# Where the hidden layer's combinations are made: behind the pair, or within the next pair's products

## The chip, the core and the metric

The kernel runs on one core of a Trainium2 chip. A core has a matrix engine (TensorE, PE in the profile, with its weight loads as PEld), a vector engine (VectorE, DVE), an activation engine (ScalarE, ACT), a general engine (GpSimd, POOL) and a queue engine (SyncE, SP), which here issues the DMAs. Each engine runs its own instructions in order, and they wait for one another by semaphores. The metric is the device time of one execution, in microseconds.

## The reference

One layer of an encoder is applied to two groups of tokens, a sample (512 tokens) and a prompt (1024 tokens), each with 16 meta tokens in front:

```python
def encoder_layer(x, w_in, ..., g_mlp, w_up, w_down):
    h = rmsnorm(x, g_mix)
    z = h @ w_in
    ...
    x = x + mixed @ w_out
    a = jax.nn.relu(rmsnorm(x, g_mlp) @ w_up)
    return x + (a * a) @ w_down
```

The change concerns `a` and `a * a` for the prompt: 1024 tokens of 1024 channels, times W_up (1024 by 4096), then relu and square.

## The kernel before

**Arithmetic.** Matrices are in 32-bit floats. Each operand is split into a rounded part (hi) and a rest (lo), and a product is the sum of three matmuls, hi·hi, hi·lo and lo·hi (`mm3`). For the prompt, both multiplications of the MLP are made by blocks of two by two with seven block products instead of eight (the scheme of Strassen and Winograd). The blocks' sums and differences have to be made: those of the normalised input and of the weights before the products, and those of the products after them.

**The class `Halves`** does this for the prompt. The tokens are two halves of 512 (TH), the channels two halves of 512. `up` (L1370) goes over 16 pairs of blocks of W_up (g), 256 hidden channels each. A pair has seven products of 12 matmuls with 512 columns, in this order: b11 (bank ps_mm), s2·t2 (ps_s), s3·t3 (ps_o), s1·t1 (ps_t), b21 (into ps_mm again), s4·b22 (added into the bank of s1, ps_t) and a22·t4 (added into the bank of s3, ps_o). Below they are called b11, s2, s3, s1, b21, s4 and the last.

**Behind the products** the outputs of a pair are put together in two tiles of 128x1024, r and r_ (in the profile r_hi and r_lo, two buffers each):
- L1391, ACT: b11's bank is copied into r.
- L1394, DVE, three times: the sums with the banks of s2, s3 and s1, each written into r_. The third reads ps_t, into which s4 is then accumulated.
- L1398, ACT: relu of ps_mm after b21.
- L1401, DVE: the sum with ps_t after s4; L1404, DVE: the sum with ps_o after the last product.
- L1407 and L1408, ACT: relu of r's right half and of r_.
- L1411, DVE: the squares of r and of r_, in place; L1412, SP: each is stored to DRAM.
- L1417, DVE: four combinations (h) of the quarters of r and r_, 128x512 each, which are operands of the block products of W_down; L1419, SP: two DMAs that store them. The two tiles of h have one buffer each.

**The weights of the next pair** are made beside the products. `prepare` (L1338) is a generator whose steps `up` takes between the products. Each step issues casts on ACT (`high`, L1286) and subtractions on POOL (`low` and `combine`, all of them L1283), and the last one the fetch of the pair after (L1280, SP). Per pair POOL has ten instructions: one of 128x1024 and nine of 128x512.

**Order.** A scheduler orders the instructions of each engine by the order of the program and by what is ready. `layer.pinned()` puts the instructions within it behind the last one traced so far on their own engine. The steps of `prepare` are pinned. The combinations are not: one of them (r's left less its right half) runs ahead of L1404 in the profile, the other three behind the square of r_.

After the loop `start_down` and `down` take over: W_down reads squares and combinations back from DRAM.

## Time and profile before

| what | us |
|---|---|
| median of three runs | 2049.44 |
| lowest and highest | 2048.82, 2049.87 |
| the profiled execution | 2049.82 |
| its span, first to last instruction | 2047.7 |
| matmuls (PE) busy in it | 1960.9 |
| DVE busy | 1131.1 |
| POOL busy | 987.6 |
| ACT busy | 756.1 |
| four combinations, first to last start | 1440.7 to 1736.9 |

The profile is of one execution. Its page gives the busy time of the engines, the span in 40 slices and the chain of work that ended last. Further views list instructions in order of time ("timeline"), who waited for whom ("waits"), and stretches of the span side by side. A row of a timeline has the start and the duration in us, the engine, the line in the kernel, the operation, what it writes and reads, shapes and count, and in brackets the idle time before it with what ended that. Tile names are the program's; since buffers are taken in turns, a weight may stand under names such as x, y or gain.

The stage with the edit takes some 310 us of the span, from 1421 to 1732 us for PE.

### The profile page before, as it was taken

The page shows a single profiled execution, that of the slowest core. Times are in us where ns is not written, and L with a number is a line of the kernel's source. Part 1 is how long each engine was busy: PE and PEld are TensorE (multiplying, and loading weights), DVE is VectorE, ACT ScalarE, POOL GpSimd, SP SyncE. Part 2 cuts the span into 40 slices and gives each one's busy share as a digit, 9 for nine tenths or more (in the row PEclk, how much of TensorE's full clock was granted, in tenths as well). Part 3 has the DMA queues.
Part 4 walks back from the last instruction along what each step waited for, and adds up shares of the span by engine and source line. Part 5 has one row for each costly group of instructions (what it writes and reads, how often), then busy time and mean ns, then how long its engine had stood idle before and what let it go on. Part 6 is the DMA issues. An engine that isn't in the chain of part 4 may idle for free.

```text
span 2047.7 us, 26413 instructions
## 1 busy us (share of the span) xinstructions
PE 1960.9 (96%) x9611; PEld 1629.3 (80%) x9611; DVE 1131.1 (55%) x1899; ACT 756.1 (37%) x1322; POOL 987.6 (48%) x758
## 2 busy tenths in 40 slices
PE   6789998999999999999999999999999999999997
PEld 4677876888888878888888888787788788888886
DVE  6573445666665543556664134657777677442246
ACT  3464323333333221555562213114333333433342
POOL 3343535367667751333334225203787885544442
PEclk9889999999999999999999999999999999999999
DMA  6554783245543444545555544312445444976663
GB/s 207 159 138 161 210 244 100 96 133 168 179 147 124 158 166 169 162 116 131 148 178 167 132 111 149 114 62 83 161 148 195 148 171 165 315 236 203 195 192 123
DMA packets 275363, 325.97 MB, mean 159 GB/s; under 512 B 42840, under 2 KB 197208, under 8 KB 274680
## 3 DMA queue, kind: packets, MB, share of 16 engines
q1 hardware_dynamic: 261504, 303.40, 46.5%
q0 software_dynamic: 13728, 20.88, 4.3%
q8 instruction: 76, 1.25, 0.3%
q14 instruction: 55, 0.45, 0.1%
HBM read 235.41 MB, written 91.37 MB: 160 GB/s over the span
## 4 chain that ended last, share of the span: by engine, by line
PE 82%; DVE 7%; DMA 3%; issue 3%; POOL 2%; ACT 2%; SPq 1%; DVEq 0%; ACTq 0%; POOLq 0%
PE ps_mm L128 22%; PE ps_o L128 20%; PE ps_s L128 18%; PE ps_t L128 7%; PE ps_mm L487 3%; PE ps_mm L488 3%; PE ps_mm L489 3%; PE ps_o L617 2%; PE ps_t L600 1%; DVE hn L863 1%; DVE gate L868 1%; POOL w_lo L152 1%; DMA w_raw<-in_w_out 1%; PE ps_t L193 1%; PE ps_s L587 1%
## 5 line engine op out<-in xcount | busy, mean ns | idle before, releaser
L152 POOL TENSOR_TENSOR w_lo<-w_raw,w_hi 128x1024 fp32r<-128x1024 f32 x99 | 248.0, 2511 | 291.3 <-ACT w_hi L151 258.0
L151 ACT CAST w_hi<-w_raw 128x1024 fp32r<-128x1024 f32 x100 | 104.7, 1048 | 170.8 <-PE ps_s L128 48.1
L1046 DVE TENSOR_TENSOR relu<-relu 128x512 f32<-128x512 f32 (+1 forms) x34 | 67.1, 1974 | 108.3 <-ACT relu L1045 108.2
L487 PE MATMUL ps_mm<-hT,w_hi 128*128 128x512 f32 (+3 forms) x312 | 122.7, 393 | 0.0
L489 PE MATMUL ps_mm<-hT,w_lo 128*128 128x512 f32 (+3 forms) x312 | 113.2, 363 | 0.0
L488 PE MATMUL ps_mm<-hT,w_hi 128*128 128x512 f32 (+3 forms) x312 | 113.2, 363 | 0.0
L1283 POOL TENSOR_TENSOR x<-w_hi,x 128x512 fp32r<-128x512 f32 (+1 forms) x42 | 78.5, 1870 | 22.8 <-ACT x L1286 22.8
L594 ACT ACTIVATE sc<-sc,ast 128x288 f32<-128x288 f32 (+4 forms) x96 | 53.8, 561 | 79.5 <-DVE ast L592 79.2
L152 POOL TENSOR_TENSOR w_lo<-r,w_hi 128x1024 fp32r<-128x1024 f32 x15 | 36.0, 2400 | 95.1 <-ACT w_hi L151 95.1
L617 PEld LDWEIGHTS ps_o<-pt,vb 104*64 104x64 f32 (+6 forms) x576 | 64.4, 169 | 12.0 <-ACT pt L132 3.8
L617 PE MATMUL ps_o<-pt,vb 104*64 104x128 f32 (+6 forms) x576 | 66.8, 252 | 5.7 <-ACT pt L132 2.9
L557 POOL TENSOR_TENSOR vb<-vr,vb 96x384 fp32r<-96x384 f32 (+4 forms) x48 | 47.9, 1012 | 49.7 <-ACT vb L556 49.5
L152 POOL TENSOR_TENSOR w_lo<-w_hi 128x1024 fp32r<-128x1024 f32 x18 | 46.5, 2581 | 49.8 <-ACT w_hi L151 45.8
L128 PE MATMUL ps_t<-gate,x 128*128 128x512 f32 x264 | 65.4, 397 | 2.7 <-DVE r_lo L1394 2.6
L152 POOL TENSOR_TENSOR w_lo<-w_lo,w_hi 128x1024 fp32r<-128x1024 f32 x18 | 45.9, 2550 | 45.5 <-ACT w_hi L151 45.5
L600 PE MATMUL ps_t<-ident,sc 128*104 128x128 f32 (+3 forms) x288 | 49.9, 284 | 18.7 <-DVE pt L133 14.1
L489 PEld LDWEIGHTS ps_mm<-hT,w_lo 128*128 128x128 f32 x312 | 60.1, 193 | 8.3
L592 DVE CUSTOM_DVE_ANT_0 sc<-ps_s,bm 128x288 f32<-128x288 f32 (+4 forms) x96 | 46.3, 483 | 36.5 <-PE ps_s L588 15.7
L128 PE MATMUL ps_mm<-gate,x 128*128 128x512 f32 x256 | 64.2, 395 | 0.0
L701 POOL MEMSET bm<- 64x96 f32 (+2 forms) x64 | 12.4, 194 | 105.9 <-DVE ast L592 79.9
L487 PEld LDWEIGHTS ps_mm<-hT,w_hi 128*128 128x128 f32 x312 | 60.6, 194 | 2.2
L488 PEld LDWEIGHTS ps_mm<-hT,w_hi 128*128 128x128 f32 x312 | 60.6, 194 | 2.2
(670 smaller groups left out, 5880.4 us busy)
## 6 DMA issues: line engine op xcount, KB each, us to landing
w_raw<-in_w_in SPq DMA_DIRECT2D x56, 512.0 KB
w_raw<-in_w_up SPq DMA_DIRECT2D x34, 512.0 KB
wt<-hn SPq DMA_DIRECT2D x32, 512.0 KB
hidden_prompt<-h SPq DMA_DIRECT2D x32, 512.0 KB
w_hi<-hidden_prompt SPq DMA_DIRECT2D x20, 512.0 KB
w_raw<-hidden_prompt SPq DMA_DIRECT2D x18, 512.0 KB
w_lo<-hidden_prompt SPq DMA_DIRECT2D x18, 512.0 KB
w_raw<-in_w_out SPq DMA_DIRECT2D x16, 512.0 KB
```

What stands on the lines that cost most here:

```text
L128: self.nc.tensor.matmul(out, a, b, start=(i == 0 and not more), stop=(i == len(terms) - 1), skip_group_check=more)
L151: nc.scalar.copy(out=hi, in_=raw)
L152: (lo_engine or nc.gpsimd).tensor_tensor(out=lo, in0=raw, in1=hi.bitcast(F32), op=ALU.subtract)
L487: nc.tensor.matmul(ps, a[0], b[0], start=(kt == 0), stop=False)
L488: nc.tensor.matmul(ps, a[0], b[1], start=False, stop=False)
L489: nc.tensor.matmul(ps, a[1], b[0], start=False, stop=(kt == 7))
L557: nc.gpsimd.tensor_tensor(out=lo, in0=vs, in1=hi.bitcast(F32), op=ALU.subtract)
L594: nc.scalar.activation(out=sc[:, :W], in_=sc[:, :W], func=AF.Exp, bias=st[:, 0:1], scale=-1.0, accum_out=st[:, 1:2])
L600: nc.tensor.transpose(tp[:ck, c * 128:(c + 1) * 128], sc[:, c * ck:(c + 1) * ck], self.ident)
L617: nc.tensor.matmul(po[:m, j * 128:(j + 1) * 128], v, x, start=(i == 0), stop=(i == len(ops) - 1))
L1046: nc.vector.tensor_tensor(out=r, in0=r, in1=r, op=ALU.mult)
L1283: self.nc.gpsimd.tensor_tensor(out=to, in0=x, in1=y, op=op)
```

## The change

The four combinations and their two stores move from the end of a pair's turn into a function of their own, `combine_hidden`. A pair puts its r, r_ and DRAM place on a list. In the next pair's turn, the first pass of the loop over s2, s3 and s1 calls the function right behind the first L1394 sum (that of s2). The call takes the entry off the list, so the two other passes do nothing. The sixteenth pair's combinations are made behind the loop. Within the function everything is pinned: the combinations come behind the last DVE instruction traced, which is that first sum, and the stores behind the last one on SP. No instruction, shape or buffer changes.

```diff
     def up(self, mp):
         layer, nc, TH = self.layer, self.nc, self.TH
+        late = []
         for g in range(self.NF // 2):
...
                 bank[k] = layer.psum(tag)
                 self.product(bank[k], s[k], 0, q)
                 nc.vector.tensor_tensor(out=to, in0=acc, in1=bank[k], op=ALU.add)
+                for _ in late[:1]:
+                    self.combine_hidden(*late.pop())
                 step()
...
             for i, x in enumerate((r, r_)):
                 nc.vector.tensor_tensor(out=x, in0=x, in1=x, op=ALU.mult)
                 nc.sync.dma_start(to[:, i * 2 * TH:(i + 1) * 2 * TH], x)
+            late.append((r, r_, to))
+        self.combine_hidden(*late.pop())
+
+    def combine_hidden(self, r, r_, to):
+
+        nc, TH = self.nc, self.TH
+        left, right = slice(0, TH), slice(TH, 2 * TH)
+        with self.layer.pinned():
             h = [self.tile(f"h{i}") for i in range(2)]
             s1, s2, s3, s4 = (x[:, y] for x in h for y in (left, right))
             for k, x, y, op in ((s1, r[:, right], r_[:, right], ALU.add), (s2, s1, r[:, left], ALU.subtract),
                                 (s3, r[:, left], r[:, right], ALU.subtract), (s4, r_[:, left], s2, ALU.subtract)):
                 nc.vector.tensor_tensor(out=k, in0=x, in1=y, op=op)
             for i, x in enumerate(h, 2):
                 nc.sync.dma_start(to[:, i * 2 * TH:(i + 1) * 2 * TH], x)
```

## The prediction, made before the change was run

> **What bounds the kernel now.** I read the page first: its line of engines and its chain.

> ```profile
> PE 1960.9 (96%) x9611; PEld 1629.3 (80%) x9611; DVE 1131.1 (55%) x1899; ACT 756.1 (37%) x1322; POOL 987.6 (48%) x758
> PE 82%; DVE 7%; DMA 3%; issue 3%; POOL 2%; ACT 2%; SPq 1%; DVEq 0%; ACTq 0%; POOLq 0%
> ```

> TensorE (PE) is busy 96% of the span and is 82% of the chain, so a change on VectorE (DVE) counts only where PE waits for DVE. The edited stage, W_up of the prompt, has the combinations (L1417) from 1440.7 to 1737.6 us. Next come two stretches of it (columns: us, then busy us and count of PE, weight loads, DVE, ACT, POOL, then granted clock, DMA share, GB/s) and, for 1425 to 1745 us, all waits of PE and of its weight loads, as total, times, longest.

> ```profile
> 1440.00:1460.00 20.00, 17.36 (x75) 13.73 (x74) 15.28 (x14) 6.62 (x10) 15.97 (x10) 1.00 0.43 154
> 1480.00:1500.00 20.00, 20.00 (x88) 16.08 (x87) 14.23 (x11) 6.82 (x11) 16.01 (x10) 1.00 0.45 159
> ...
> PE ps_t L128 <- DVE r_lo L1394: 2.6, 1, 2.6
> PEld ps_t L128 <- DVE r_lo L1394: 4.7, 8, 3.1
> ```

> PE is full except in the stage's second pair (1440 to 1460), where it waits once, 2.6 us, for a sum of L1394; seven more weight loads share the other 1.6 us (4.7 - 3.1). So this edit can win about 3 us at most, and can lose wherever it makes the third L1394 sum later: PE's sixth product of a pair accumulates into the bank which that sum reads (ps_t). The timelines of one undisturbed pair give the clockwork; PE first, then DVE:

> ```profile
> 1496.42 2.96 PE L128 MATMUL ps_mm<-gate,x 128*128 128x512 f32 x12
> ...
> 1507.62 2.96 PE L128 MATMUL ps_mm<-gate,x 128*128 128x512 f32 x12
> 1510.42 2.95 PE L128 MATMUL ps_t<-gate,y 128*128 128x512 f32 x12
> ...
> 1495.24 1.99 DVE L1411 TENSOR_TENSOR r_hi<-r_hi 128x1024 f32<-128x1024 f32 x1 [0.70 <-ACT r_hi L1407]
> 1497.26 1.66 DVE L1417 TENSOR_TENSOR h<-r_hi 128x512 f32<-128x512 f32 x1
> 1498.84 0.68 DVE L1404 TENSOR_TENSOR r_lo<-r_lo,ps_o 128x512 f32<-128x512 f32 x1
> 1500.64 1.23 DVE L1411 TENSOR_TENSOR r_lo<-r_lo 128x1024 f32<-128x1024 f32 x1 [1.13 <-ACT r_lo L1408]
> 1501.90 2.77 DVE L1417 TENSOR_TENSOR h<-r_hi,r_lo 128x512 f32<-128x512 f32 x1
> 1504.70 1.67 DVE L1417 TENSOR_TENSOR h<-h,r_hi 128x512 f32<-128x512 f32 x1
> 1506.40 1.67 DVE L1417 TENSOR_TENSOR h<-r_lo,h 128x512 f32<-128x512 f32 x1
> 1507.99 0.67 DVE L1394 TENSOR_TENSOR r_lo<-r_hi,ps_s 128x512 f32<-128x512 f32 x1
> 1508.77 0.69 DVE L1394 TENSOR_TENSOR r_lo<-r_lo,ps_o 128x512 f32<-128x512 f32 x1
> 1509.56 0.69 DVE L1394 TENSOR_TENSOR r_lo<-r_lo,ps_t 128x512 f32<-128x512 f32 x1
> ```

> Products start every 2.80 us (1510.42 - 1507.62): b11 1496.42, then s2 1499.22, s3 1502.02, s1 1504.82, b21 1507.62, s4 1510.42, the last 1513.21, the next pair at 1516.00. DVE does the previous pair's combinations first and reaches the three sums late, the third ending at 1510.25, 0.17 us before s4 starts. Since s4's weight load is among those that waited, while the product itself is on its 2.80, this is just in time: **slack zero**.

> Why do combinations take 1.67 us? In the sixteenth pair, without POOL beside them, they take 0.69 (last row). GpSimd (POOL) now, the same pair as above:

> ```profile
> 1494.83 1.31 POOL L1283 TENSOR_TENSOR gain<-w_lo,gain 128x512 fp32r<-128x512 f32 x1
> ...
> 1501.62 2.49 POOL L1283 TENSOR_TENSOR y<-w_hi,x 128x1024 fp32r<-128x1024 f32 x1 [3.26 <-ACT x L1286]
> 1504.19 1.62 POOL L1283 TENSOR_TENSOR w_hi<-w_hi,w_lo 128x512 f32<-128x512 f32 x1
> 1505.89 1.62 POOL L1283 TENSOR_TENSOR w_lo<-w_lo 128x512 f32<-128x512 f32 x1
> 1507.48 1.74 POOL L1283 TENSOR_TENSOR x<-w_hi,x 128x512 fp32r<-128x512 f32 x1
> ...
> 1514.43 1.29 POOL L1283 TENSOR_TENSOR x<-w_lo,x 128x512 fp32r<-128x512 f32 x1
> 1515.67 2.27 POOL L1283 TENSOR_TENSOR x<-w_hi,x 128x512 fp32r<-128x512 f32 x1
> ...
> 1720.02 0.69 DVE L1417 TENSOR_TENSOR h<-r_lo,h 128x512 f32<-128x512 f32 x1
> ```

> POOL's instructions end at 1504.11, 1505.81 and 1507.51, the combinations at 1504.67, 1506.37 and 1508.07, always 0.56 later, and each POOL instruction then ends 1.14 after the combination. The two alternate, one combination per POOL instruction, every 1.70 us. The sums of L1394 and L1404, which read PSUM, keep 0.67 to 0.69 beside a busy POOL.

> **The change part by part.** Nothing is added or removed: 4 DVE instructions and 2 DMAs for each of 16 pairs. Fifteen times they move behind the next pair's first L1394 sum; the sixteenth stays behind the loop, where PE already runs W_down, and I cost it at nothing.

> *The tail gets longer.* Ahead of the third sum stood, behind the first blocked combination (ends 1504.67), two combinations and three sums. Now it is three combinations and two sums: the combination that ran early, at 1497.26, joins the row (+1.70) and the first sum leaves it (-0.78, from 1507.99 to 1508.77). Net **+0.92 us**.

> *The row starts earlier.* With that combination gone from between L1411 and L1404, L1404 starts earlier, and behind it ACT's relu and cast and POOL's first instruction, the 128x1024 one, which ended 5.27 us after L1404 began (1504.11 - 1498.84). How much earlier is set by what L1411 waits for. Its input comes 0.20 + 0.69 + 0.70 us after the sixth product's end; POOL's last instruction then holds it off. That one hangs on ACT:

> ```profile
> 1510.62 0.60 ACT L1398 ACTIVATE r_hi<-ps_mm 128x512 f32<-128x512 f32 x1 [3.62 <-PE ps_mm L128]
> 1511.11 0.61 ACT L1286 CAST x<-w_hi 128x512 fp32r<-128x512 f32 x1
> 1513.41 0.69 DVE L1401 TENSOR_TENSOR r_hi<-r_lo,ps_t 128x512 f32<-128x512 f32 x1 [3.16 <-PE ps_t L128]
> ```

> L1398 waits for b21's end, and the cast behind it ends at 1511.72. So POOL, which will be ahead of where it is now, stops there, starts its last three at 1511.80, 1513.05 and 1514.30 (a pitch of 1.25) and ends at 1515.60. L1411 is ready at 1514.8, waits for that, and ends 1.09 later (now 1497.23, against 1496.14 of POOL's first row), at 1516.69. L1404 starts 0.08 before this, 0.61 after the next pair's b11, where it is 2.42 now (1498.84 - 1496.42). If this pair itself stalled by x at its sixth product, the next b11 moves by x and POOL's gate does not: 0.61 - x, but not under 0.20, when L1404's own bank is finished (as L1398 starts 0.20 after s4's start).

> POOL's 128x1024 then ends at 0.61 - x + 5.27 = 5.88 - x after b11. The first sum runs from 1502.22 to 1502.89, 6.47 after b11, so the first combination misses that gap: it meets POOL's *second* instruction (0.08 + 1.29 us more), which ends at 7.25 - x. Today it waits until 7.69 (1504.11). Gain 0.44 + x, at most 0.85.

> *Per pair.* Stall = 0.92 - 0.44 - x = 0.48 - x, not under 0.07, with x the stall of the pair before: alternately 0.07 and 0.41, **mean 0.24 us**. Over 13 pairs (third to fifteenth) +3.1. In the sixteenth, combinations take 0.69 (no POOL work left), three of them fit, and nothing is lost.

> *The second pair* has its own wait now:

> ```profile
> 1440.74 0.68 DVE L1417 TENSOR_TENSOR h<-r_hi 128x512 f32<-128x512 f32 x1
> 1443.20 2.77 DVE L1417 TENSOR_TENSOR h<-r_hi,r_lo 128x512 f32<-128x512 f32 x1
> 1446.01 2.96 PE L128 MATMUL ps_mm<-gate,x 128*128 128x512 f32 x12
> 1451.61 3.06 PE L128 MATMUL ps_t<-gate,x 128*128 128x512 f32 x12 [2.64 <-DVE r_lo L1394]
> ```

> L1404 stands ahead of the combination there already, so nothing starts earlier and the full +0.92 applies: the wait becomes 3.56.

> *One hiccup* goes either way: at 1587 DVE lost 0.46 us between two sums, with no other engine as its releaser, which cost PE 0.35. I count half of that back, -0.2.

> ```profile
> 1587.45 0.69 DVE L1394 TENSOR_TENSOR r_lo<-r_lo,ps_o 128x512 f32<-128x512 f32 x1 [0.46 <-DVE r_lo L1394]
> ```

> *Queues.* The 2 DMAs of h sit on SP behind the stores of r, wait some 1.4 us longer, and have behind them only the fetch at the pair's end (about 1516), so nothing is late. POOL and ACT get no new wait. What is late next is the second and third sum, already counted.

> *Sum:* 0.92 + 3.1 - 0.2 = +3.8 us. The profiled execution took 2049.82 (span 2047.7 and 2.1 around it), so 2053.6; against the median of the three runs, 2049.44, it is **2053.3 us**. The unknown is the stall per pair. Its floor is zero, with the second pair unchanged; its ceiling is 0.92, with no earlier start. I take the recursion, as each of its terms is a row.

> *The clock.* Of the four rows below two are PE's instructions ahead of the stage, two are windows.

> ```profile
> 1408.14 0.63 PE L1170 MATMUL ps_s<-ident,h 128*128 128x128 f32 x4 [3.54 <-DVE gate L133]
> 1409.66 3.53 PE L128 MATMUL ps_mm<-gate,y 128*128 128x512 f32 x8
> ...
> 1409.00:1412.00 3.00, 3.00 (x12) 2.23 (x11) 2.58 (x9) 1.79 (x6) 1.22 (x1) 0.55 0.15 43
> 1450.00:1453.00 3.00, 1.39 (x6) 1.17 (x7) 1.38 (x2) 1.12 (x2) 2.84 (x3) 1.00 0.43 175
> ```

> After an idle 3.54 us the granted clock fell to 0.55, and 8 matmuls took 3.53 us where 8 at the stage's pace (2.80 / 12 each) take 1.9: a loss of 1.6. After the 2.64 us of the second pair it stayed 1.00. A wait of 3.56 there is on the edge; the sum leaves the drop out. [...]

> **The rivals.** *A: slower, plainly.* The row does not start earlier: L1411 falls behind one POOL instruction more, L1404 with it, and the first combination is released near 7.69 as now. For it speaks that the phase of POOL decides and can be off by one instruction (1.3 us); against it, that the 1.66 us ahead of L1404 plainly go. Price: 0.92 in 14 pairs, +12.9, 2062. It decides, that is passes 4.1 us in sum, from a mean stall of 0.26 in the 13 pairs ((4.1 - 0.92 + 0.2) / 13).

> *B: the sums are not held.* The second and third sums are not tied behind the combinations in the text, and the order is a scheduler's: it now pulls one combination ahead of L1404. If it puts those sums ahead of the last combinations, PE never waits, and the second pair's 2.6 and the 0.35 go: -3.0, 2046.5. Against: the combinations come first in program order and are ready together.

> *C: the clock.* As the forecast, but the second pair's wait trips it: +1.6, 2054.9.

> **How the numbers follow.** Forecast 0.58 (own range 2051 to 2057), A 0.14, B 0.14, C 0.14. 0.2% is 4.1 us, about what a measurement of this kernel can tell from no change, and the forecast sits just under it. Slower by more: A, most of C and some 0.38 of the forecast, 0.14 + 0.10 + 0.22 = 0.46. Faster by more: a rare B, 0.04. Within: 0.50. The range 2047 to 2060 leaves out the lower part of B and most of A.

> **What would show it.** In the changed trace: L1394's first sum ends about 6.5 us after b11 and four L1417 follow without a gap, each ending 0.56 after a POOL instruction; L1404 starts 0.2 to 0.6 after b11; the weight loads of ps_t wait for L1394 in nearly every pair, in sum 3 us more than now; the second pair's wait is about 3.5. Wrong: combinations of 0.69, a sum between them, waits of 0.9 in each pair, or a chain that gains or loses outside 1430 to 1740.

## The result and the profile after

| | before | changed |
|---|---|---|
| median, us (22 runs each) | 2049.93 | 2055.26 |
| lowest to highest | 2045.46 to 2055.08 | 2050.38 to 2057.48 |
| the profiled execution, and its span | 2049.82, 2047.7 | 2055.41, 2053.6 |
| the edited stage in that profile | 296.90 | 302.93 |

The ratio of changed to before is 1.0018, with a 95% interval of 1.0011 to 1.0025: 2.3 to 5.1 us more, 3.7 in the middle. That is slower, by about 0.2%. (The medians lie 5.33 apart and the means 4.00. Single runs of either kernel spread over 7 to 10 us, so the text goes by the ratio and its interval.)

The stage's length runs from the second pair's first matmul (b11) to the first matmul of W_down: 1434.82 to 1731.72 us before, 1434.74 to 1737.67 after. It grew by 6.03, and the rest of the span by nothing (what follows it took 315.98 and 315.93). This length, and the length of a pair (b11 to b11), carry the study. Undisturbed pairs repeat to some hundredths between profiles, while the same stage begins anywhere from 1432.6 to 1439.1 in the profiles of kernels that are alike up to there.

The page of the changed kernel, its lines of engines and of the chain's shares:

```profile
PE 1966.6 (96%) x9611; PEld 1631.1 (79%) x9611; DVE 1104.3 (54%) x1899; ACT 758.8 (37%) x1322; POOL 977.3 (48%) x758
PE 80%; DVE 9%; DMA 3%; issue 3%; ACT 2%; POOL 2%; SPq 1%; DVEq 0%; ACTq 0%; POOLq 0%
```

DVE is busy 27 us less (it was 1131.1) and the kernel is slower: DVE's share of the chain rose from 7 to 9%. The combination of r and r_, first of the four in the stage's groups by line, shows where the busy time went (columns: count, then total and mean ns, idle before); before, then changed:

```profile
L1417 DVE TENSOR_TENSOR h<-r_hi,r_lo 128x512 f32<-128x512 f32 x16 | 40.1, 2507 | 0.6
```
```profile
L1428 DVE TENSOR_TENSOR h<-r_hi,r_lo 128x512 f32<-128x512 f32 x16 | 17.9, 1119 | 0.0
```

It took 2.77 us in the pair of the prediction, where it takes 0.69 without POOL beside it: it was held some 2.1 us by POOL's 128x1024 instruction, counted as busy. Now it starts later and meets a short one. From the third pair on, being held there had cost PE next to nothing: with one exception those pairs took 19.56 to 19.59, and in third_sum below, where nothing waits, they take 19.58.

The waits of the stage (1425 to 1750 us), as total, times, longest:

```profile
PEld ps_t L128 <- DVE r_lo L1395: 9.4, 15, 3.9
...
PE ps_t L128 <- DVE r_lo L1395: 3.5, 1, 3.5
```

The sums of L1394 are L1395 now. Weight loads wait for them in 15 pairs instead of 8, and the one wait of PE has grown from 2.6 to 3.5 us. The same two stretches as before, and then two short ones:

```profile
1440.00:1460.00 20.00, 16.49 (x60) 12.82 (x59) 12.27 (x12) 6.61 (x10) 15.25 (x10) 0.83 0.41 148
1480.00:1500.00 20.00, 19.89 (x86) 15.73 (x85) 12.60 (x12) 6.50 (x10) 15.41 (x11) 1.00 0.46 159
```
```profile
1448.24:1451.66 3.42, 0.66 (x3) 0.19 (x1) 3.29 (x3) 0.60 (x1) 3.34 (x3) 1.00 0.37 153
1451.66:1455.07 3.41, 2.66 (x6) 2.15 (x7) 0.69 (x1) 1.76 (x3) 3.33 (x4) 0.50 0.37 154
```

The granted clock, 1.00 in the first stretch before, is 0.83, and 0.50 in the row that starts at 1451.66, where the second pair's wait ends. The products there, b21 and s4 of the second pair, show the price:

```profile
1445.94 2.96 PE L128 MATMUL ps_mm<-gate,x 128*128 128x512 f32 x12
...
1452.41 5.49 PE L128 MATMUL ps_t<-gate,x 128*128 128x512 f32 x12 [3.51 <-DVE r_lo L1395]
```

The twelve matmuls of s4 take 5.49 us, where they took 3.06 before. The lengths of the pairs:

| pair | before | changed | changed, profiled again |
|---|---|---|---|
| second | 22.46 | 26.10 | 24.89 |
| third to fifteenth | 19.56 to 19.59, one 19.90 | 19.66 or 19.67 and 19.93, alternately | 19.62 to 19.66 and 19.93 to 19.95, alternately |
| sixteenth | 19.58 | 19.58 | 19.58 |

A pair of the changed kernel (b11 at 1500.43) and the start of the one before it (b11 at 1480.50), PE, then DVE, then POOL:

```profile
1480.50 2.02 PE L128 MATMUL ps_mm<-gate,gain 128*128 128x512 f32 x8
...
1500.43 2.96 PE L128 MATMUL ps_mm<-gate,x 128*128 128x512 f32 x12
...
1511.62 2.96 PE L128 MATMUL ps_mm<-gate,x 128*128 128x512 f32 x12
1514.42 3.06 PE L128 MATMUL ps_t<-gate,y 128*128 128x512 f32 x12
```
```profile
1481.03 0.68 DVE L1407 TENSOR_TENSOR r_lo<-r_lo,ps_o 128x512 f32<-128x512 f32 x1
...
1499.24 1.50 DVE L1414 TENSOR_TENSOR r_hi<-r_hi 128x1024 f32<-128x1024 f32 x1 [0.70 <-ACT r_hi L1410]
1500.67 0.67 DVE L1407 TENSOR_TENSOR r_lo<-r_lo,ps_o 128x512 f32<-128x512 f32 x1
...
1506.28 0.69 DVE L1395 TENSOR_TENSOR r_lo<-r_hi,ps_s 128x512 f32<-128x512 f32 x1 [2.59 <-PE ps_s L128]
1506.88 0.98 DVE L1428 TENSOR_TENSOR h<-r_hi,r_lo 128x512 f32<-128x512 f32 x1
1507.79 1.78 DVE L1428 TENSOR_TENSOR h<-r_hi 128x512 f32<-128x512 f32 x1
1509.49 1.77 DVE L1428 TENSOR_TENSOR h<-h,r_hi 128x512 f32<-128x512 f32 x1
1511.30 1.67 DVE L1428 TENSOR_TENSOR h<-r_lo,h 128x512 f32<-128x512 f32 x1
1512.90 0.68 DVE L1395 TENSOR_TENSOR r_lo<-r_lo,ps_o 128x512 f32<-128x512 f32 x1
1513.68 0.69 DVE L1395 TENSOR_TENSOR r_lo<-r_lo,ps_t 128x512 f32<-128x512 f32 x1
```
```profile
1503.45 2.50 POOL L1283 TENSOR_TENSOR y<-w_hi,x 128x1024 fp32r<-128x1024 f32 x1 [3.78 <-ACT x L1286]
1506.02 1.29 POOL L1283 TENSOR_TENSOR w_hi<-w_hi,w_lo 128x512 f32<-128x512 f32 x1
1507.39 1.63 POOL L1283 TENSOR_TENSOR w_lo<-w_lo 128x512 f32<-128x512 f32 x1
1508.98 1.74 POOL L1283 TENSOR_TENSOR x<-w_hi,x 128x512 fp32r<-128x512 f32 x1
1510.80 1.63 POOL L1283 TENSOR_TENSOR w_hi<-w_lo,w_hi 128x512 f32<-128x512 f32 x1
```

The four combinations (L1428) stand without a gap behind the first sum, each ending 0.54 or 0.55 us after one of POOL's second to fifth (the first 1507.86 and 1507.31, the last 1512.97 and 1512.43). The second and third sums wait behind them, though their banks were filled long before: s3 ended 8.4 us after b11 began (three products of 2.80), at 1508.8, and its sum begins at 1512.90. The third ends at 1514.37, 0.05 before s4 starts.

### The profile page after: what moved, and what is told of

Same layout as the page of the kernel before. It is cut to its first block, busy times and chain, and to the rows that moved or that the text cites. A ratio compares the mean times of both kernels' runs of the same rounds, so it can differ in the third digit from the quotient of the medians.

```text
span 2053.6 us, 26398 instructions
## 1 busy us (share of the span) xinstructions
PE 1966.6 (96%) x9611; PEld 1631.1 (79%) x9611; DVE 1104.3 (54%) x1899; ACT 758.8 (37%) x1322; POOL 977.3 (48%) x758
## 3 DMA queue, kind: packets, MB, share of 16 engines
q8 instruction: 76, 1.25, 0.3%
## 4 chain that ended last, share of the span: by engine, by line
PE 80%; DVE 9%; DMA 3%; issue 3%; ACT 2%; POOL 2%; SPq 1%; DVEq 0%; ACTq 0%; POOLq 0%
PE ps_mm L128 21%; PE ps_o L128 20%; PE ps_s L128 18%; PE ps_t L128 7%; PE ps_mm L487 3%; PE ps_mm L488 3%; PE ps_mm L489 3%; DVE h L1428 2%; PE ps_o L617 2%; PE ps_t L600 1%; DVE hn L863 1%; DVE gate L868 1%; POOL w_lo L152 1%; DVE gate L862 1%; PE ps_t L193 1%
## 5 line engine op out<-in xcount | busy, mean ns | idle before, releaser
L1283 POOL TENSOR_TENSOR x<-w_hi,x 128x512 fp32r<-128x512 f32 (+1 forms) x42 | 69.2, 1648 | 29.4 <-ACT x L1286 28.7
L128 PE MATMUL ps_t<-gate,x 128*128 128x512 f32 x264 | 68.7, 411 | 4.0 <-DVE r_lo L1395 3.5
L128 PEld LDWEIGHTS ps_t<-gate,x 128*128 128x128 f32 x264 | 50.3, 194 | 19.7 <-DVE r_lo L1395 8.3
L592 DVE CUSTOM_DVE_ANT_0 sc<-ps_s,bm 128x288 f32<-128x288 f32 (+4 forms) x96 | 46.3, 482 | 33.4 <-PE ps_s L588 15.6
L128 PE MATMUL ps_mm<-gate,x 128*128 128x512 f32 x256 | 64.2, 395 | 0.0
L488 PEld LDWEIGHTS ps_mm<-hT,w_hi 128*128 128x128 f32 x312 | 60.0, 192 | 2.2
```

Source lines behind the costliest of these rows:

```text
L128: self.nc.tensor.matmul(out, a, b, start=(i == 0 and not more), stop=(i == len(terms) - 1), skip_group_check=more)
L488: nc.tensor.matmul(ps, a[0], b[1], start=False, stop=False)
L1283: self.nc.gpsimd.tensor_tensor(out=to, in0=x, in1=y, op=op)
```

## The experiments

The theory: the third sum is late by the row of DVE instructions ahead of it, as the prediction worked it out, and behind the second pair's wait the clock falls besides. The main rivals: the loss sits in a wait elsewhere, or in the clock alone. All edits below are made to the changed kernel; where an edit moves lines, the rows have the edited kernel's numbers.

**again: the changed kernel once more.** No edit.

> The changed kernel once more, for the runs beside it. Stage length here means: from the second pair's b11 to the first matmul of W_down in the profile (before 296.9 us, changed 302.9). My theory: the wait of the second pair is 3.5 us again and the weight loads of ps_t wait in nearly every pair, so the stage is at least 300.1 (296.9 + 0.8 + 2.4). Whether the clock falls behind the 3.5 us is open: with the drop the stage is 302.9 again, without it about 300.1. Rival: the drop belongs to the change and comes in every execution, then the time is 5 to 6 us above before; if it comes in some, 3 to 6.

Measured, in 5 rounds: 1.0024 (1.0015 to 1.0033), 2055.47 beside 2050.59. Its stage took 301.68 us. The second pair's s4:

```profile
1451.59 4.40 PE L128 MATMUL ps_t<-gate,x 128*128 128x512 f32 x12 [3.50 <-DVE r_lo L1395]
```

The wait is the same to 0.01, and the clock fell again, with a smaller price: the second pair is 2.43 longer than before (24.89 - 22.46), of which 0.87 is the wait, so 1.56 is the clock; in the first profile it was 3.64 - 0.87 = 2.77.

**third_sum: the combinations behind the third sum instead of the first.**

```diff
-                for _ in late[:1]:
+                for _ in late[:k == "s1"]:
                     self.combine_hidden(*late.pop())
```

> Combinations behind the third L1395 sum instead of the first; nothing else. My theory: only the sums that stand behind the combinations cost PE anything, so no wait of PE or of a weight load is left in the stage, in the second pair either, and no clock drop: 15 pairs of 19.58 us, stage 293.7, time 3 us under before (2.8 + 0.35). L1404 and the squares come later by up to 2 us, which PE doesn't see. Rival, that making the combinations inside the next pair costs by itself (POOL held off, stores later, pins): stage near 300 or more, time above before.

Measured, in 5 rounds: **0.9981 (0.9972 to 0.9990)**, 2047.54 us. This is faster than both kernels, by 3.9 us (2.1 to 5.7) against the one before. The stage took 293.70 us, and every pair 19.58. Of its waits that concern ps_t's sum, DVE's timeline and PE's s4:

```profile
PEld ps_t L128 <- DVE r_lo L1395: 0.3, 1, 0.3
```
```profile
1523.48 0.69 DVE L1395 TENSOR_TENSOR r_lo<-r_lo,ps_o 128x512 f32<-128x512 f32 x1 [2.06 <-PE ps_o L128]
1526.28 0.69 DVE L1395 TENSOR_TENSOR r_lo<-r_lo,ps_t 128x512 f32<-128x512 f32 x1 [2.11 <-PE ps_t L128]
1526.88 1.60 DVE L1428 TENSOR_TENSOR h<-r_hi,r_lo 128x512 f32<-128x512 f32 x1
...
1531.92 1.66 DVE L1428 TENSOR_TENSOR h<-r_lo,h 128x512 f32<-128x512 f32 x1
1533.50 0.68 DVE L1404 TENSOR_TENSOR r_hi<-r_lo,ps_t 128x512 f32<-128x512 f32 x1
```
```profile
1528.88 2.96 PE L128 MATMUL ps_t<-gate,x 128*128 128x512 f32 x12
```

The brackets turn the story round: the sums now wait for PE, each about 2.1 us, and the third ends at 1526.97, 1.91 us before s4 starts. The combinations are still held by POOL (1.6 to 1.7 us in these rows) and cost nothing: what stands behind them, L1404, reads s4's result, and no wait for it is listed on PE. So their duration costs PE something only where the third sum stands behind them. The clock alone is excluded too: pairs three to fifteen, which had no drop, go from 19.66 and 19.93 to 19.58.

**pair2_only: the second pair alone is relieved.**

```diff
-                for _ in late[:1]:
+                for _ in late[:g > 1 or k == "s1"]:
                     self.combine_hidden(*late.pop())
```

> As the changed kernel, but in the second pair alone the combinations come behind the third sum. My theory: the second pair's wait and the clock drop behind it go (its length from 26.1 to 19.6 us), the small waits of the later pairs stay (2.4 us): stage 296.4, time about that of before, within 1 us, and 3.5 to 6.4 under the changed kernel. Rival, that the wait is only handed to the third pair: stage 299 or more.

Measured, in 5 rounds: 0.9998 (0.9988 to 1.0008), no difference from before. The second pair took 19.58, but the stage 298.22, between the 296.4 of the theory and the rival's 299: the third pair took 21.47. Its POOL and PE:

```profile
1457.84 3.04 POOL L1283 TENSOR_TENSOR y<-w_hi,gain 128x1024 fp32r<-128x1024 f32 x1 [0.29 <-ACT gain L1286]
```
```profile
1452.18 2.02 PE L128 MATMUL ps_mm<-gate,y 128*128 128x512 f32 x8
...
1467.98 2.36 PE L128 MATMUL ps_t<-gate,x 128*128 128x512 f32 x9 [1.64 <-DVE r_lo L1395]
```

POOL's 128x1024 instruction ends 8.70 after this pair's b11 (1460.88 - 1452.18), where the pair of the prediction had 7.69. By the prediction's row the lateness is 0.92 + 1.01 = 1.93; s4 came 1.80 late. So about half of what the second pair lost to its wait in the changed kernel (6.47 - 2.80 = 3.67) is handed to the third. The row of POOL starts 0.29 after the one before it ended: it is still behind with its work, and the wait in the second pair had given it time to catch up (in the changed kernel it sits idle for 5.44 us ahead of the third pair's 128x1024 instruction). Behind the wait of 1.64 the first nine matmuls of s4 took 2.36 us, the pace of 3.06 for twelve: no drop.

**cast_first: ACT casts s2's weights before the relu of b21, not behind it.**

```diff
-                nc.scalar.activation(out=r[:, left], in_=a, func=AF.Relu)
                 step()
+                nc.scalar.activation(out=r[:, left], in_=a, func=AF.Relu)
```

> As the changed kernel, but the cast of s2 is issued on ACT ahead of the relu that waits for b21 (the two change places), so POOL's last three instructions don't hang on b21. My theory of the alternation: L1414 ends some 0.4 us earlier, L1407 always starts at its floor (0.2 after b11), and the stalls no longer alternate between 0.07 and 0.4 but are all near 0.07: the stage is 1.5 to 2 us shorter than in the changed kernel. Rival, that the alternation comes from elsewhere: the stalls still alternate and the stage is unchanged.

Measured, in 5 rounds: 1.0011 (1.0000 to 1.0021). By these times alone it can't be told from "again", whose interval overlaps; the profiles tell them apart. The alternation is gone: pairs three to fifteen took 19.64 to 19.67. The stage, 299.99, is 1.69 shorter than in "again", with the same second pair (24.90). ACT's cast and relu (L1402 here), and DVE's square and sum with ps_o around the next b11, which starts at 1497.54:

```profile
1489.91 0.62 ACT L1286 CAST x<-w_hi 128x512 fp32r<-128x512 f32 x1 [2.75 <-POOL w_hi L1283]
...
1492.10 0.60 ACT L1402 ACTIVATE r_hi<-ps_mm 128x512 f32<-128x512 f32 x1 [1.57 <-PE ps_mm L128]
```
```profile
1496.36 1.30 DVE L1414 TENSOR_TENSOR r_hi<-r_hi 128x1024 f32<-128x1024 f32 x1 [0.70 <-ACT r_hi L1410]
1497.74 0.69 DVE L1407 TENSOR_TENSOR r_lo<-r_lo,ps_o 128x512 f32<-128x512 f32 x1
```

The cast no longer waits for b21's end, so POOL's last instructions come earlier and the square is not held. L1407 starts 0.20 after b11 here, and the stall is the floor of the recursion (0.07): the gate that the prediction named, ACT's relu ahead of the cast, is what made pairs alternate.

**split: one combination goes back to the place it had.** The difference of r's halves is made behind its own pair, unpinned; the other three stay behind the next pair's first sum.

```diff
-            late.append((r, r_, to))
+            h = [self.tile(f"h{i}") for i in range(2)]
+            nc.vector.tensor_tensor(out=h[1][:, left], in0=r[:, left], in1=r[:, right], op=ALU.subtract)
+            late.append((r, r_, to, h))
...
             for k, x, y, op in ((s1, r[:, right], r_[:, right], ALU.add), (s2, s1, r[:, left], ALU.subtract),
-                                (s3, r[:, left], r[:, right], ALU.subtract), (s4, r_[:, left], s2, ALU.subtract)):
+                                (s4, r_[:, left], s2, ALU.subtract)):
```

> The combination of r's left and right half stays behind its own pair, unpinned, as before the change; the three others come behind the first sum. My theory: the row ahead of the third sum is three combinations and two sums, one sum (0.78 us) less than before, and starts as before, since L1407 is held by that combination again: no wait in the pairs from the third on, the second pair's wait 0.8 shorter (1.9 us), no clock drop: stage 295.7, time 1 us under before. Rival, that the place behind the first sum costs by itself: waits of 0.07 to 0.4 in the later pairs as in the changed kernel, stage 297 or more.

Measured, in 3 rounds: 0.9986 (0.9974 to 0.9999). From the third pair on every pair took 19.58. In the pair with b11 at 1501.49 the third sum ends at 1513.78, 1.70 before s4. So the combination that joined the row was the one too many, as the +1.70 said. In the second pair PE waited 1.84 and then lost another 1.55 on s4:

```profile
1455.09 4.61 PE L128 MATMUL ps_t<-gate,x 128*128 128x512 f32 x12 [1.84 <-DVE r_lo L1395]
```
```profile
1452.50:1455.91 3.41, 1.57 (x8) 0.96 (x7) 2.44 (x3) 0.67 (x2) 3.33 (x3) 1.00 0.75 308
1455.91:1459.33 3.42, 3.42 (x10) 2.65 (x9) 0.00 (x0) 1.76 (x3) 3.34 (x4) 0.50 0.00 0
```

The clock was 0.50 and the product took 4.61 instead of 3.06: the stage, 297.35 against 295.7 expected, is longer by about this. Here a wait of 1.84 us was followed by a drop, which no earlier reading had suggested. The profiled execution, 2054.28, was also the slowest of the ten (median 2048.61).

**second_sum: the combinations behind the second sum.** The condition is `late[:k == "s3"]`.

> Combinations behind the second L1395 sum. My theory (what counts is how many combinations and sums stand ahead of the third sum, and when the first of them may start): the second sum ends 9.28 us after b11, the four combinations end 0.6 to 1.9 + 5.1 us later, so the third ends at 15.6 to 16.9 where PE needs it by 13.8: a wait of 1.8 to 3.0 us in 14 pairs, stage 25 to 42 us longer than the 293.7 without waits, time 2070 to 2090. In the second pair POOL sets the row's start as in the changed kernel, its wait is 2.6 to 3.5. Rival, that the place within the pair matters little and the changed kernel's loss is POOL's delay: stage 298 to 303.

One profile: the stage took 323.98, 30.3 more than third_sum's, and PE waited for the third sum in all 15 pairs. (Two executions were made. The profile is of one, 2075.91; the other took 7122.61 with a mean clock of 0.27, and nothing is read from it.) The second, third and fourth pair's s4:

```profile
1451.04 3.07 PE L128 MATMUL ps_t<-gate,x 128*128 128x512 f32 x12 [2.70 <-DVE r_lo L1395]
...
1473.21 4.61 PE L128 MATMUL ps_t<-gate,x 128*128 128x512 f32 x12 [2.33 <-DVE r_lo L1395]
...
1496.24 3.07 PE L128 MATMUL ps_t<-gate,x 128*128 128x512 f32 x12 [1.64 <-DVE r_lo L1395]
```

The combinations start one product (2.80) later than in the change, and the row behind them is one sum (0.78) shorter; s4 is some 1.8 late in most pairs instead of 0.2. So the place decides, and not by degrees: in pairs three to fifteen the loss is 2.7 us behind the first sum, 26.6 (1.6 of it the clock) behind the second, and none behind the third. Of the clock: no drop after 2.70, one after 2.33.

**clock_doses and clock_same: graded waits for the clock.** To third_sum, scratch additions on DVE are added ahead of the third sum of five pairs, so that s4 waits 2.4 to 3.6 us, or 3.1 each time.

```diff
+                if k == "s1":
+                    with layer.pinned():
...
+                        for m in [TH] * full + [n] * (n > 0):
+                            nc.vector.tensor_tensor(out=self.tile("h0")[:, :m], in0=r_[:, :m], in1=bank["s3"][:, :m], op=ALU.add)
```

> Combinations behind the third sum, where no wait is left, and additions into a scratch tile on DVE ahead of the third sum of the pairs 3, 6, 9, 12 and 15, so that PE idles there for about 2.4, 2.7, 3.0, 3.3 and 3.6 us. [...]

> The same with an idle of about 3.1 us in each of the pairs 3, 6, 9, 12 and 15. [...]

Both failed to make the waits. The only wait of PE for such an addition in clock_doses:

```profile
PE ps_o L128 <- DVE h L1399: 0.4, 1, 0.4
```

Only the additions were pinned, and PE's products were put into another order around them. The two took 2046.08 and 2048.65 us, one execution each; nothing follows for the clock.

**wait_short and wait_long: the same with PE's order held.** Each product is now placed behind the one before it on PE, and the three sums are pinned too; the subtractions are sized for waits of 2.7 (wait_short) and 3.4 to 3.5 us (wait_long).

```diff
-        self.layer.mm3(ps, [...], **kw)
+        with self.layer.behind(self.layer.mark((mybir.EngineType.PE,))):
+            self.layer.mm3(ps, [...], **kw)
```

> The doses again, with PE's products and the third sum kept in their order, so that PE waits: combinations behind the third sum, and in the pairs 3, 6, 9, 12 and 14 subtractions into a scratch tile on DVE ahead of the third sum, for an idle of PE of about 2.7 us each. If the clock falls by a fixed length of idle time, all five go one way. [...]

> The same with an idle of about 3.4 to 3.5 us, that of the changed kernel's second pair. [...]

wait_short gave five waits, all of 3.57 and not 2.7:

```profile
1476.98 4.61 PE L128 MATMUL ps_t<-gate,x 128*128 128x512 f32 x12 [3.57 <-DVE r_lo L1400]
...
1541.09 3.06 PE L128 MATMUL ps_t<-gate,x 128*128 128x512 f32 x12 [3.57 <-DVE r_lo L1400]
```

The third, fourth and fifth took 4.61, 4.42 and 4.55. Five equal waits in the same surroundings, four with a drop and one without: something besides the wait's length decides. In wait_long's one execution, 3012 us, the granted clock was 0.55 to 0.65 for nearly the whole span, so its times don't compare. What set waits with and without a drop apart is read from the traces in the last section.

## Why the prediction came out as it did

It named 2053.3 us, 3.8 more than before; measured was 3.7 more (2.3 to 5.1), with a median of 2055.26. The mechanism was right and so were nearly all terms, but the sum is closer than its steps: one was left out that should have stood in it.

- **Slack zero, and what can be won.** Right. third_sum frees the sums and gains 3.20 us in the stage (296.90 - 293.70): 2.88 of the second pair and 0.32 of the hiccup. That is the "about 3 us at most" for this edit, and the outcome that rival B described.
- **The tail, +0.92.** In the second pair, where nothing else moves, s4 starts 6.47 after b21 instead of 5.60: +0.87. split, which takes the one joined combination out again, removes the stall from the third pair on.
- **The row starts earlier, 0.61 - x.** L1407 started 0.53 after b11 where the pair before had lost 0.08, and 0.24 (1500.67 - 1500.43) where it had lost 0.35; the forms give 0.53 and 0.26. POOL's 128x1024 instruction ended 5.52 after b11 (1505.95 - 1500.43), against 5.53. cast_first moved ACT's cast, which the formula names as the gate, and got its floor.
- **Per pair, 0.07 and 0.41, mean 0.24.** Measured 0.08 and 0.35, mean 0.21: 2.7 in 13 pairs instead of 3.1.
- **The sixteenth pair at nothing.** Right: 19.58 in both. The combinations behind the loop cost nothing that the 315.9 us behind the stage show.
- **The hiccup, -0.2.** It didn't come back: -0.32, all of it.
- **What would show it.** The first sum ended 6.54 after b11 (1506.97 - 1500.43; 6.5 named), and the combinations behind it ran as described. The weight loads' waits grew by 4.7 in sum (9.4 - 4.7), where 3 were named: the second pair's own is 0.8 of it.
- **The clock: the step that failed.** The prediction put the wait at 3.56, measured as 3.51, and then "the sum leaves the drop out". The clock fell in all three profiles with this wait (changed, again, cast_first), for 2.77, 1.56 and 1.57 us. Rival C's price, +1.6, was right; its place, beside the sum with a chance of 0.14, was not. No run shows that a drop behind such a wait is the rarer outcome. The trace before the change already had a wait of 3.54 upstream with a drop behind it, and 3.56 is no shorter. In split even 1.84 us was followed by one (last section). Laid out by the stretches of 3.413 us that the last section reads from the clock's records, the 3.54 lay as 1.29 and 2.25 us in two of them, parted at 1405.89, and the drop followed; the second pair's 2.64 before the change lay as 1.29 and 1.35, and the clock stayed at 1.00.

The first profile's sum: 0.87 + 2.71 - 0.32 + 2.77 = 6.03, which is what the stage grew by. Without the clock the terms give 3.26, with the smaller drop 4.8. The measured 3.7 (2.3 to 5.1) and again's 4.9 (3.1 to 6.8) hold both, so the timed runs can't say whether the clock falls in each of their executions; only the profiled ones show it. The nearness of 3.8 to 3.7 therefore proves the order of size and not each term: terms that came out 0.54 lower in sum stand against a clock term that was missing. That they nearly cancel is luck.

How large the missing term is on average can be estimated, if the place of those stretches against the stage is taken as random, and 1.84 us of idle time within one, split's reading, as what brings a drop. Then a wait of 3.51 escapes it in (2 x 1.84 - 3.51) / 3.41 = 5% of executions, and the 2.64 of the kernel before in 30%. By this estimate the kernel before would pay for a drop too in most executions, though it did not in the one that was profiled, and the change would make drops more frequent only by (3.51 - 2.64) / 3.41, a quarter. At the smaller price that is 0.25 x 1.56 = 0.4 us, and 3.26 + 0.4 = 3.7. This fits what was measured, but it is an estimate: one profile of the kernel before doesn't show it.

Rival A fell: L1407 started early in each pair read, and the 13 pairs lost 0.21 and not 0.92. Rival B fell for the change itself: the second and third sums stayed behind the combinations (why the scheduler left them there, no run shows); but the same edit two sums later makes it true.

## What to carry to other kernels

When work is moved behind an instruction on an in-order engine, ask which instruction behind it frees a buffer that the bounding engine needs next, and move the work behind that one: here two sums further turned 3.7 us lost into 3.9 won, with the same instructions. An engine's busy time is no cost by itself: DVE's fell by 27 us in the slower kernel. And where a wait of the bounding engine grows near a length at which a row of the same trace shows its clock falling, put the drop into the sum with that row's price, and ask whether the shorter wait before the change would pay it in other executions too.

## What the runs showed of the hardware that was not expected

```profile
1446.85:1450.26 3.41, 2.12 (x10) 1.36 (x8) 3.27 (x4) 1.74 (x3) 3.33 (x3) 1.00 0.39 162
1450.26:1453.67 3.41, 2.06 (x9) 1.70 (x10) 1.19 (x2) 1.56 (x3) 3.25 (x4) 1.00 0.35 145
```
```profile
1535.94:1539.36 3.41, 1.58 (x7) 0.94 (x5) 3.24 (x6) 1.80 (x4) 2.59 (x3) 1.00 0.00 0
1539.36:1542.77 3.41, 1.68 (x7) 1.41 (x8) 3.35 (x5) 0.34 (x1) 3.41 (x3) 1.00 0.05 13
```

PE was idle (the first number less the second) for 1.29 and 1.35 us in the first two, for 1.83 and 1.73 in the others, and the clock stayed at 1.00. It was idle for 1.84 in split's from 1452.50 (3.41 - 1.57), for 2.76 in the changed kernel's from 1448.24 (3.42 - 0.66), and upstream in the kernel before for 2.25 from 1405.89 (3.41 - 1.16); behind each of these three the clock was 0.50. The length of a wait orders none of this: 2.70 had no drop (second_sum, s4 in 3.07), 2.33 (there too, 4.61) and 1.84 (split, 4.61) had one. This is read afterwards, from profiles not made for it, and the 1.83 without a drop and the 1.84 with one are too close to tell apart.
- **In split the drop cost 1.55 us, behind a wait of 1.84.** The product behind a drop took 4.40 to 4.61 us, and 5.49 in the changed kernel's first profile, instead of 3.06. In that profile the clock stayed at 0.50 for two stretches (6.83 us), and 0.76 us of the wait lay in the first of them (1451.655 to 1452.41); in split, with one (1455.91 to 1459.33), PE was busy for all of it.
